# Attention weights and V split in two parts each: three fp32r matmuls where one fp32 matmul stood

## The chip, the cores and the metric

One core of a Trainium2 chip runs the whole program. The metric is the device time of one execution in microseconds (us). Three runs of the kernel before took 3181.44, 3177.22 and 3178.43 us; the median is 3178.43 us.

## The reference, cut to what matters

Two layers of a hybrid block over 256 context and 1024 latent tokens, width 1024. Each layer projects the normalised tokens once and feeds three mixers side by side: a Fourier mixing, grouped-query attention (8 query heads, 2 key and value heads of width 64) and a gated linear recurrence (HGRN2); a SwiGLU follows. The change is in this part:

```python
def attend(q, k, v):
    s = jnp.einsum('bkgqd,bksd->bkgqs', q, k).astype(jnp.float32) * (HEAD_DIM ** -0.5)
    p = jax.nn.softmax(s, axis=-1).astype(v.dtype)
    return jnp.einsum('bkgqs,bksd->bkgqd', p, v)
```

Everything is fp32. The latent queries read all 1280 keys; the context queries (layer 0 alone) read the 256 context keys.

## The kernel before, in words

Activations lie with channels on partitions and tokens along the free axis, in blocks of 256 (context), 512 and 512 tokens. Most products are made of two parts per operand: a number is cast to fp32r (the high part), the rest after the cast is the low part, and three fp32r matmuls high·high, high·low and low·high are summed in PSUM (`mm3`, L131 to L133). `split` (L124, L125) makes the parts: ScalarE casts, VectorE subtracts. A few products are single fp32 matmuls, among them `pv`, the product of the exponentials with V (L639).

A layer first runs its projections in order: some gates, the values (`values`, L533), the keys (`keys`, L512 to L518), the queries of four head pairs (`queries`, L562, L563), the other gates. Each block of keys and queries passes `qk_norm_rope`: ScalarE squares it into `qsq` (L470) and scales it into `qraw` (L472), TensorE sums squares (`qss`, L476), ScalarE makes the reciprocal root `qr` in two steps (L311, L312), VectorE turns the block by `sin` and `cos` (L483 to L485). Then a query is multiplied by `qr` and stored to DRAM by a DMA on SyncE's queue (L562, L563); a key is multiplied into `kro` (L512) and split from there into the tiles K1 and K2 of two groups (L516 to L518). In layer 0 VectorE also adds up modulation vectors in the background meanwhile (L274, tiles `as` and `wa`).

Then come the attention units, one for a head pair and a block of queries: twelve in layer 0 (eight of ten steps, four of two), eight of ten steps in layer 1, so 168 steps. A step takes 128 keys: four matmuls `sc` (L630, L631) for two heads, two exponentials on ScalarE (L633), and the two `pv` matmuls of the step before it. Between them stand pieces of other work, handed out at a fixed rate: the next unit's row maxima (`mx`, L597, reduced on VectorE), the recurrence (`lp`, `kv`, `ho` and others) and the Fourier mixing (`pq`, `fo`).

A scheduler puts all instructions in one order for each engine and hands out the buffers of each pool in turn. Two pools matter: `five` has 25 slots of 128x1280 fp32, and `t2` has five slots of 128x512 (`qsq`, `qraw`, `qr` and `kro` among others). While the queries are made, the slots of `five` hold 16 tiles of the normalised tokens (high and low), 2 of V, `cos` and `sin`, and 4 of K1 and K2: 24 in all.

Of the kernel before, what the change touches and what calls it, by code (L numbers as in the profile page):

```python
# [10 lines left out]
F32 = mybir.dt.float32  # L11
F32R = mybir.dt.float32r
U8 = mybir.dt.uint8
AF = mybir.ActivationFunctionType
ALU = mybir.AluOpType
# [3 lines left out]
P = 128  # L19
# [80 lines left out]
class Kern:  # L100
# [434 lines left out]
    def values(self, l):  # L535

        nc = self.nc
        W = 384
        wh, wl = self.wv

        self.V = [self.five(f"V{l}_{g}", shape=(P, 10, P)) for g in range(2)]
        for V in self.V:
            nc.gpsimd.memset(V[:, :, 64:P], 1.0)
        for t in range(10):
            acc = self.ps("mm", f"v{l}_{t}")
            ts = slice(t * P, (t + 1) * P)
            self.mm3(acc[:, :W], [(self.hh[k][:, ts], self.hl[k][:, ts], wh[k], wl[k]) for k in range(KD)])
            for g in range(2):
                nc.scalar.copy(out=self.V[g][:, t, 0:64], in_=acc[:, 64 * g:64 * g + 64])
            vi = self.t2("vi")  # L550
            nc.vector.tensor_copy(out=vi[:, 0:256], in_=acc[:, P:W])
            nc.sync.dma_start(out=self.dv[t], in_=vi[:, 0:256])
# [62 lines left out]
    def unit_attend(self, l, j, ci, Q1, Q2):  # L615


        nc = self.nc
        g = j // 2
        n = CHUNKS[ci][1]  # L620
        nk = 2 if ci == 0 else 10
        pv = [self.ps("pv", f"pv{j}_{ci}_{a}") for a in range(2)]
        ps = []
        for kt in range(nk + 1):
            if kt < nk:
                ks = slice(kt * P, (kt + 1) * P)
                p = []
                for a in range(2):
                    sc = self.ps("sc", "sc")
                    nc.tensor.matmul(sc[:, :n], self.K1[g][:, ks], Q1[a], start=True, stop=False)  # L630
                    nc.tensor.matmul(sc[:, :n], self.K2[g][0:66, ks], Q2[a][0:66], start=False, stop=True)  # L631
                    pf = self.t2(f"p{a}", tag="pa", bufs=PAB)[:, :n]
                    nc.scalar.activation(out=pf, in_=sc[:, :n], func=AF.Exp, scale=0.125)  # L633
                    p.append(pf)
                ps.append(p)
            if kt:
                i = kt - 1
                for a in range(2):
                    nc.tensor.matmul(pv[a][:, :n], self.V[g][:, i], ps[i][a], start=(i == 0), stop=(i == nk - 1))  # L639
            if kt == DELAY and self.pending:  # L640
                self.pending()
                self.pending = None
            yield
        if self.pending:
            self.pending()
        pvs, r = [self.t2(nm, tag="acc", bufs=ACB)[:, :n] for nm in ("pvs", "lns")]
        for a in range(2):
            nc.scalar.copy(out=pvs[64 * a:64 * a + 64], in_=pv[a][0:64, :n])
            nc.scalar.activation(out=r[64 * a:64 * a + 64], in_=pv[a][64:P, :n], func=AF.Ln)
        self.pending = lambda: self.unit_finish(j, ci, pvs, r)  # L650
# [871 lines left out]
```

## Time and profile before

| | |
|---|---|
| median of three runs | 3178.43 us |
| profiled execution | 3176.16 us, span 3174.2 us |
| granted clock | 0.986 of full speed |
| TensorE (PE) busy | 3048.2 us, 96% |
| VectorE (DVE) busy | 1976.1 us, 62% |
| ScalarE (ACT) busy | 1414.2 us, 45% |
| GpSimd (POOL) busy | 114.0 us, 4% |
| attention of layer 0 | first `pv` 347.8 us, last 731.6 us |
| attention of layer 1 | first `pv` 2018.0 us, last 2367.0 us |

The profiled execution lies 2.3 us under the median; about 2 us lie outside its span. Shares of busy time are means over stages with different limits, so each stage is read by its own window. A matmul of fp32 stands in the rows as two records, and the record of a matmul is longer than its distance to the next one, because matmuls are pipelined: the distance between two starts tells what one costs.

### The profile page before, as it was taken

The numbers are of one execution on the slowest core, as the hardware profiler recorded it, in microseconds if no ns is written. First come the engines' busy times: TensorE is split into PE (matmuls) and PEld (weight loads), VectorE is DVE, ScalarE is ACT, GpSimd is POOL, SyncE is SP. The second block draws the span as 40 slices with busy tenths as digits, with TensorE's granted clock in tenths as the row PEclk, the third lists the DMA queues.
The fourth block names the chain that finished last, engine by engine and source line by source line (L and its number), as shares of the span: only waits on it lengthen the run. The fifth ranks groups of instructions, "written<-read, shape, count | busy, mean of one in ns | idle before, by whom it ended". The sixth has DMA issues, their size and how long they took to land.

```text
span 3174.2 us, 43396 instructions
## 1 busy us (share of the span) xinstructions
PE 3048.2 (96%) x16114; PEld 2378.9 (75%) x16114; DVE 1976.1 (62%) x3457; ACT 1414.2 (45%) x2578; POOL 114.0 (4%) x89
## 2 busy tenths in 40 slices
PE   7999999999889999998998999999999799999998
PEld 4877666667768888886888897665668588887887
DVE  5299877663777766665537427777544866666343
ACT  6255555563542323333425535545563433334343
POOL 1000000000210000000001000000001100000000
PEclk9999999999999999998999999999999899999999
DMA  8346201135223333347735423211243122225452
GB/s 290 97 155 206 89 25 67 30 122 172 87 83 100 110 126 111 96 134 231 220 113 179 143 94 105 67 59 36 73 141 118 58 80 81 85 80 189 139 170 93
DMA packets 358651, 369.41 MB, mean 116 GB/s; under 512 B 21896, under 2 KB 268072, under 8 KB 358440
## 3 DMA queue, kind: packets, MB, share of 16 engines
q1 hardware_dynamic: 358440, 366.65, 36.4%
q8 instruction: 126, 2.06, 0.3%
q14 instruction: 85, 0.70, 0.1%
HBM read 282.00 MB, written 84.41 MB: 115 GB/s over the span
## 4 chain that ended last, share of the span: by engine, by line
PE 81%; DVE 8%; ACT 4%; DMA 4%; issue 2%; SPq 1%; POOL 0%; DVEq 0%; ACTq 0%; POOLq 0%
PE fp L131 8%; PE fp L133 8%; PE fp L132 8%; PE pv L639 7%; PE fd L131 5%; PE fd L132 5%; PE fd L133 5%; PE u L131 3%; PE u L132 3%; PE u L133 3%; PE mx L597 2%; PE sc L630 2%; PE sc L631 2%; PE oacc L132 2%; PE oacc L131 2%; PE oacc L133 2%
## 5 line engine op out<-in xcount | busy, mean ns | idle before, releaser
L131 PE MATMUL fd<-a,hwd 128*128 128x512 f32 (+1 forms) x880 | 328.3, 373 | 16.5 <-ACT hwd L124 16.5
L133 PE MATMUL fd<-a,lwd 128*128 128x512 f32 (+1 forms) x880 | 327.9, 373 | 8.9 <-DVE lwd L125 8.9
L132 PE MATMUL fd<-a,hwd 128*128 128x512 f32 (+1 forms) x880 | 327.0, 372 | 0.0
L125 DVE TENSOR_TENSOR lwd<-rwd,hwd 128x512 fp32r<-128x512 f32 (+1 forms) x240 | 158.1, 661 | 269.1 <-ACT hwd L124 260.3
L639 PE MATMUL pv<-p,V 128*128 128x512 f32 (+1 forms) x672 | 316.0, 584 | 0.0
L124 ACT CAST hwd<-rwd 128x512 fp32r<-128x512 f32 (+1 forms) x240 | 140.3, 585 | 306.6 <-PE fd L132 178.7
L598 DVE TENSOR_REDUCE mp<-mx 128x1 f32<-128x512 f32 (+1 forms) x400 | 220.7, 589 | 69.2 <-PE mx L597 66.1
L633 ACT ACTIVATE p<-sc 128x512 f32<-128x512 f32 (+1 forms) x336 | 184.1, 585 | 132.5 <-PE sc L631 128.7
L131 PEld LDWEIGHTS fd<-a,hwd 128*128 128x128 f32 x880 | 168.9, 192 | 45.1 <-ACT hwd L124 17.4
L133 PEld LDWEIGHTS fd<-a,lwd 128*128 128x128 f32 x880 | 168.3, 191 | 38.4 <-DVE lwd L125 10.9
L132 PEld LDWEIGHTS fd<-a,hwd 128*128 128x128 f32 x880 | 168.9, 192 | 27.7 <-issue 0.2
L274 DVE SCALAR_TENSOR_TENSOR as<-wa,sc,as 128x512 f32<-128x512 f32 x224 | 161.1, 747 | 36.3 <-DMA wa<-in_w_ada_dram 34.9
L639 PEld LDWEIGHTS pv<-p,V 128*128 128x128 f32 x672 | 122.7, 189 | 77.9 <-issue 62.7
L131 PE MATMUL fp<-mh,hw_gate 128*128 128x512 f32 x352 | 141.2, 401 | 6.1 <-ACT hw_gate L124 6.0
L133 PE MATMUL fp<-mh,lw_gate 128*128 128x512 f32 x352 | 139.5, 396 | 5.8 <-DVE lw_gate L125 5.8
L132 PE MATMUL fp<-ml,hw_gate 128*128 128x512 f32 x352 | 139.4, 396 | 1.2 <-POOL ml L1051 1.2
L131 PE MATMUL fp<-mh,hw_up 128*128 128x512 f32 x352 | 137.8, 392 | 0.0
L132 PE MATMUL fp<-ml,hw_up 128*128 128x512 f32 x352 | 137.8, 391 | 0.0
L133 PE MATMUL fp<-mh,lw_up 128*128 128x512 f32 x352 | 137.2, 390 | 0.0
L131 PE MATMUL u<-a0hh,hwin 128*128 128x512 f32 (+1 forms) x360 | 132.3, 370 | 3.9 <-ACT a0hh L327 2.1
L132 PE MATMUL u<-a0hl,hwin 128*128 128x512 f32 (+1 forms) x360 | 129.1, 359 | 5.5 <-POOL a0hl L325 3.8
L133 PE MATMUL u<-a0hh,lwin 128*128 128x512 f32 (+1 forms) x360 | 127.3, 355 | 0.0
(353 smaller groups left out, 7376.8 us busy)
## 6 DMA issues: line engine op xcount, KB each, us to landing
rwd<-in_w_down_dram SPq DMA_DIRECT2D x200, 256.0 KB
wa<-in_w_ada_dram SPq DMA_DIRECT2D x192, 256.0 KB
rw_gate<-in_w_gate_dram SPq DMA_DIRECT2D x44, 512.0 KB
rw_up<-in_w_up_dram SPq DMA_DIRECT2D x44, 512.0 KB
da<-mw_gate SPq DMA_DIRECT2D x88, 256.0 KB
ar<-da SPq DMA_DIRECT2D x88, 256.0 KB
rwin<-in_w_in_dram SPq DMA_DIRECT2D x30, 512.0 KB
rwo<-in_w_out_dram SPq DMA_DIRECT2D x24, 512.0 KB
```

The lines of the kernel that those rows point to most:

```text
L124: self.nc.scalar.copy(out=hi, in_=src)
L125: self.nc.vector.tensor_tensor(out=lo, in0=src, in1=hi, op=ALU.subtract)
L131: self.nc.tensor.matmul(out, lh, rh, start=(first and i == 0), stop=False)
L132: self.nc.tensor.matmul(out, lh, rl, start=False, stop=False)
L133: self.nc.tensor.matmul(out, ll, rh, start=False, stop=(last and i == n - 1))
L274: nc.vector.scalar_tensor_tensor(out=acc, in0=w, scalar=sc, in1=acc, op0=ALU.mult, op1=ALU.add)
L597: nc.tensor.matmul(mx[:, :kn], Q1[a][:, t * P:(t + 1) * P], self.K1[g][:, k0:k0 + kn])
L598: nc.vector.tensor_reduce(out=mp[:, a * nt + t, i:i + 1], in_=mx[:, :kn], axis=AX.X, op=ALU.max)
L630: nc.tensor.matmul(sc[:, :n], self.K1[g][:, ks], Q1[a], start=True, stop=False)
L631: nc.tensor.matmul(sc[:, :n], self.K2[g][0:66, ks], Q2[a][0:66], start=False, stop=True)
L633: nc.scalar.activation(out=pf, in_=sc[:, :n], func=AF.Exp, scale=0.125)
L639: nc.tensor.matmul(pv[a][:, :n], self.V[g][:, i], ps[i][a], start=(i == 0), stop=(i == nk - 1))
```

## The change

V is kept as a high and a low tile per group (four tiles of the pool `five` per layer in place of two; the columns of ones that make the sums of the exponentials get zeros in the low part). `split` fills them: to ScalarE's copy of 128x64 comes a subtract on VectorE, 40 times. Each exponential tile gets a cast on ScalarE and a subtract on GpSimd, 336 times each, written to a new tile `ps` from `five`; `mm3` then replaces the matmul L639. After the edit lines below L546 move by one, those below L635 by four.

```diff
--- before.py
+++ after.py
@@ -538,15 +538,16 @@
         W = 384
         wh, wl = self.wv
 
-        self.V = [self.five(f"V{l}_{g}", shape=(P, 10, P)) for g in range(2)]
+        self.V = [[self.five(f"V{p}{l}_{g}", F32R, (P, 10, P)) for p in "hl"] for g in range(2)]
         for V in self.V:
-            nc.gpsimd.memset(V[:, :, 64:P], 1.0)
+            for v, x in zip(V, (1.0, 0.0)):
+                nc.gpsimd.memset(v[:, :, 64:P].bitcast(F32), x)
         for t in range(10):
             acc = self.ps("mm", f"v{l}_{t}")
             ts = slice(t * P, (t + 1) * P)
             self.mm3(acc[:, :W], [(self.hh[k][:, ts], self.hl[k][:, ts], wh[k], wl[k]) for k in range(KD)])
             for g in range(2):
-                nc.scalar.copy(out=self.V[g][:, t, 0:64], in_=acc[:, 64 * g:64 * g + 64])
+                self.split(acc[:, 64 * g:64 * g + 64], *[v[:, t, 0:64] for v in self.V[g]])
             vi = self.t2("vi")
             nc.vector.tensor_copy(out=vi[:, 0:256], in_=acc[:, P:W])
             nc.sync.dma_start(out=self.dv[t], in_=vi[:, 0:256])
@@ -631,12 +632,15 @@
                     nc.tensor.matmul(sc[:, :n], self.K2[g][0:66, ks], Q2[a][0:66], start=False, stop=True)
                     pf = self.t2(f"p{a}", tag="pa", bufs=PAB)[:, :n]
                     nc.scalar.activation(out=pf, in_=sc[:, :n], func=AF.Exp, scale=0.125)
-                    p.append(pf)
+                    y = self.five(f"ps{a}", F32R, (P, 2, 512))
+                    p.append([y[:, i, :n] for i in range(2)])
+                    nc.scalar.copy(out=p[a][0], in_=pf)
+                    nc.gpsimd.tensor_tensor(out=p[a][1], in0=pf, in1=p[a][0], op=ALU.subtract)
                 ps.append(p)
             if kt:
                 i = kt - 1
                 for a in range(2):
-                    nc.tensor.matmul(pv[a][:, :n], self.V[g][:, i], ps[i][a], start=(i == 0), stop=(i == nk - 1))
+                    self.mm3(pv[a][:, :n], [(*[v[:, i] for v in self.V[g]], *ps[i][a])], i == 0, i == nk - 1)
             if kt == DELAY and self.pending:
                 self.pending()
                 self.pending = None
```

The four tiles of V, with the others, make 26 tiles for the 25 slots while the queries are made. The first place is ScalarE in layer 1, where the keys end and the queries begin; K_1_1 is K1 or K2 of the second group, K_1_0 of the first. Before:

```order
L472 ACTIVATE qraw<-u_256_1_17320,colv 128x512
L516 CAST K_1_0_17163<-kro 64x512
L518 CAST K_1_0_17165<-kro 64x512
L516 CAST K_1_1_17164<-kro 64x512
L518 CAST K_1_1_17166<-kro 64x512
L311 ACTIVATE qr<-qss,eps 128x512
L124 CAST hwin_512_0_17505<-rwin_512_17503 128x4x64
L312 ACTIVATE qr<-qr 128x512
L124 CAST hwin_512_0_17505<-rwin_512_17503 128x4x64
L124 CAST hwin_512_4_17511<-rwin_512_17503 128x4x64
```

After, the same place:

```order
L124 CAST hwin_384_4_18345<-rwin_384_18337 128x4x64
L312 ACTIVATE qr<-qr 128x512
L516 CAST K_1_0_18091<-kro 64x512
L518 CAST K_1_0_18093<-kro 64x512
L518 CAST K_1_1_18094<-kro 64x512
L470 ACTIVATE qsq<-u_256_1_18248 128x512
L472 ACTIVATE qraw<-u_256_1_18248,colv 128x512
L124 CAST hwin_512_0_18433<-rwin_512_18431 128x4x64 x2
```

and the end of the last query:

```order
L311 ACTIVATE qr<-qss,eps 128x512
L312 ACTIVATE qr<-qr 128x512
L470 ACTIVATE qsq<-u_640_2_18579 128x512
L472 ACTIVATE qraw<-u_640_2_18579,colv 128x512
L516 CAST K_1_1_18092<-kro 64x256
L516 CAST K_1_1_18092<-kro 64x512 x2
L311 ACTIVATE qr<-qss,eps 128x512
L312 ACTIVATE qr<-qr 128x512
L674 ACTIVATE lsa<-u_1152_0_18629 128x256
```

The cast into K1 of the second group (L516) moved from beside the other three to a place behind the last query's `qsq` and `qraw`; it stands there three times (x2 counts two blocks), with its subtract on VectorE (L517). The slot that it waits for is that of `sin`. In layer 0 it is the same.

The second place is VectorE in layer 0's queries, one block of 512 from the product with `qr` to the rope of the next. Before:

```order
L125 TENSOR_TENSOR lwin_640_4_2161<-rwin_640_2152,hwin_640_4_2160 128x4x64
L276 TENSOR_SCALAR as_2049<-wa_0_6_1828,sc_149 128x512
L276 TENSOR_SCALAR as_2050<-wa_0_7_1874,sc_149 128x512
L276 TENSOR_SCALAR as_2051<-wa_0_7_1874,sc_149 128x512
L274 SCALAR_TENSOR_TENSOR as_2049<-wa_1_6_1890,sc_149,as_2049 128x512
L483 TENSOR_TENSOR qsq<-qraw,sin_1489 64x512 x2
L274 SCALAR_TENSOR_TENSOR as_2050<-wa_1_7_1918,sc_149,as_2050 128x512
L484 TENSOR_TENSOR qraw<-qraw,cos_1488 128x512
L305 SCALAR_TENSOR_TENSOR mod_495<-adat_2027,colv 128x4
L485 TENSOR_TENSOR qraw<-qraw,qsq 128x512
L305 SCALAR_TENSOR_TENSOR mod_495<-adat_2027,colv 128x4
L562 TENSOR_TENSOR qraw<-qraw,qr 128x512
```

After:

```order
L563 TENSOR_TENSOR qraw<-qraw,qr 128x512
L274 SCALAR_TENSOR_TENSOR as_2072<-wa_7_6_2306,sc_149,as_2072 128x512
L274 SCALAR_TENSOR_TENSOR as_2073<-wa_7_6_2306,sc_149,as_2073 128x512
L274 SCALAR_TENSOR_TENSOR as_2074<-wa_7_7_2322,sc_149,as_2074 128x512
L274 SCALAR_TENSOR_TENSOR as_2075<-wa_7_7_2322,sc_149,as_2075 128x512
L276 TENSOR_SCALAR as_2604<-wa_0_8_2364,sc_149 128x512
L274 SCALAR_TENSOR_TENSOR as_2604<-wa_1_8_2431,sc_149,as_2604 128x512
L483 TENSOR_TENSOR qsq<-qraw,sin_1513 64x512 x2
L274 SCALAR_TENSOR_TENSOR as_2604<-wa_2_8_2484,sc_149,as_2604 128x512
L484 TENSOR_TENSOR qraw<-qraw,cos_1512 128x512
L274 SCALAR_TENSOR_TENSOR as_2604<-wa_3_8_2633,sc_149,as_2604 128x512
L485 TENSOR_TENSOR qraw<-qraw,qsq 128x512
```

More of the modulation sums (L274) stand between two blocks of queries. Between the first and the last query's product stand 69 rows of L274 and L276 now, before it was 44; later, among the gates, stand 32 where 60 stood.

The third place is the end of the last unit of layer 0, on TensorE. Before:

```order
L639 MATMUL pv_2_0_6900<-p_6990,V_1_1185 128x512
L639 MATMUL pv_2_1_6901<-p_6995,V_1_1185 128x512
L630 MATMUL sc<-Q_6264,K_0_1_1493 128x512
L631 MATMUL sc<-Q_6265,K_0_1_1495 128x512
L630 MATMUL sc<-Q_6264,K_0_1_1493 128x512
L631 MATMUL sc<-Q_6265,K_0_1_1495 128x512
L639 MATMUL pv_2_0_6900<-p_7002,V_1_1185 128x512
L639 MATMUL pv_2_1_6901<-p_7007,V_1_1185 128x512
L639 MATMUL pv_2_0_6900<-p_7014,V_1_1185 128x512
L639 MATMUL pv_2_1_6901<-p_7019,V_1_1185 128x512
```

After:

```order
L131 MATMUL pv_2_0_7704<-ps_7884,Vh_1_1186 128x512
L132 MATMUL pv_2_0_7704<-ps_7884,Vh_1_1186 128x512
L133 MATMUL pv_2_0_7704<-ps_7884,Vl_1_1187 128x512
L131 MATMUL pv_2_1_7705<-ps_7892,Vh_1_1186 128x512
L132 MATMUL pv_2_1_7705<-ps_7892,Vh_1_1186 128x512
L133 MATMUL pv_2_1_7705<-ps_7892,Vl_1_1187 128x512
L131 MATMUL pv_2_0_7704<-ps_7906,Vh_1_1186 128x512
L131 MATMUL pv_2_1_7705<-ps_7914,Vh_1_1186 128x512
L132 MATMUL pv_2_0_7704<-ps_7906,Vh_1_1186 128x512
L133 MATMUL pv_2_0_7704<-ps_7906,Vl_1_1187 128x512
L132 MATMUL pv_2_1_7705<-ps_7914,Vh_1_1186 128x512
L133 MATMUL pv_2_1_7705<-ps_7914,Vl_1_1187 128x512
```

and ScalarE there, after:

```order
L634 ACTIVATE p_7882<-sc 128x512
L634 ACTIVATE p_7890<-sc 128x512
L637 CAST ps_7884<-p_7882 128x512
L637 CAST ps_7892<-p_7890 128x512
L634 ACTIVATE p_7904<-sc 128x512
L634 ACTIVATE p_7912<-sc 128x512
L637 CAST ps_7906<-p_7904 128x512
L637 CAST ps_7914<-p_7912 128x512
```

Two `sc` pairs still stand ahead of the products of the step before. In each step ScalarE's two casts follow its two exponentials, and at the unit's end no `sc` follows, and the low part of the last tile is an operand of the last matmul but one.

## Rows read from the trace of the kernel before

**Rows 1.** the page, TensorE's busy time (share of the span, instructions)

```profile
PE 3048.2 (96%) x16114; PEld 2378.9 (75%) x16114; DVE 1976.1 (62%) x3457; ACT 1414.2 (45%) x2578; POOL 114.0 (4%) x89
```

**Rows 2.** layer 0's attention by form: count | busy, mean ns | idle

```profile
L639 PE MATMUL pv<-p,V 128*128 128x512 f32 x320 | 154.8, 594 | 0.0
...
L633 ACT ACTIVATE p<-sc 128x512 f32<-128x512 f32 x158 | 88.6, 595 | 63.6 <-PE sc L631 62.5
```

**Rows 3.** one line, the product with V: ns min/median/max, first and last start

```profile
L639 PE MATMUL pv<-p,V x672: 377/592/697, 347.8 to 2368.2; 128*128 128x512 f32 x160, 128*128 128x256 f32 x8
```

**Rows 4.** chain of waits near 650 us: start, us, what

```profile
649.96 1.72 PE pv L639 x4
```

**Rows 5.** timeline of TensorE, end of layer 0's attention: start, us, what

```profile
712.41 1.88 PE L639 MATMUL pv<-p,V 128*128 128x512 f32 x4
...
714.37 0.39 PE L631 MATMUL sc<-Q,K 66*128 66x512 f32 x1
...
714.60 0.40 PE L630 MATMUL sc<-Q,K 128*128 128x512 f32 x1
...
715.07 1.88 PE L639 MATMUL pv<-p,V 128*128 128x512 f32 x4
...
729.87 3.60 PE L639 MATMUL pv<-p,V 128*128 128x512 f32 x8
```

**Rows 6.** windows: length, busy PE, PEld, DVE, ACT, POOL, clock, DMA share, GB/s

```profile
110.00:165.00 55.00, 54.72 (x309) 52.69 (x308) 14.60 (x31) 12.29 (x40) 0.00 (x0) 1.00 0.30 97
192.00:255.00 63.00, 61.47 (x302) 48.56 (x302) 62.21 (x109) 31.83 (x62) 0.00 (x0) 1.00 0.54 168
255.00:345.00 90.00, 88.44 (x446) 71.31 (x447) 77.19 (x144) 49.30 (x91) 0.41 (x1) 1.00 0.60 200
340.00:740.00 400.00, 390.75 (x2715) 250.90 (x2715) 275.10 (x596) 242.40 (x449) 4.55 (x4) 1.00 0.24 77
1900.00:1963.00 63.00, 62.83 (x270) 48.63 (x268) 47.99 (x78) 35.81 (x66) 0.00 (x0) 1.00 0.24 76
```

**Rows 7.** TensorE's waits in layer 0's attention: us in total, times, longest

```profile
PE sc L630 <- ACT p L633: 3.0, 4, 1.3
```

**Rows 8.** ScalarE's groups by form, the cast of 128x512

```profile
L124 ACT CAST hwd<-rwd 128x512 fp32r<-128x512 f32 x200 | 124.0, 620 | 240.0 <-PE fd L132 122.1 <-DMA rwd<-in_w_down_dram 100.0 <-PE fd L133 9.1
```

**Rows 9.** GpSimd's groups by form, two inputs of 128x512

```profile
L392 POOL TENSOR_TENSOR sqa<-sqa,sq 128x512 f32<-128x512 f32 x20 | 29.0, 1452 | 346.1 <-ACT sq L391 346.1
L1096 POOL TENSOR_TENSOR xT<-xT,xT 128x512 f32<-128x512 f32 x8 | 16.5, 2070 | 37.6 <-ACT xT L1046 37.6
L1051 POOL TENSOR_TENSOR ml<-xT,mh 128x512 fp32r<-128x512 f32 x8 | 13.5, 1694 | 0.1
```

**Rows 10.** timeline of VectorE, one block of queries in layer 1

```profile
1909.61 1.39 DVE L483 TENSOR_TENSOR qsq<-qraw,sin 64x512 f32<-64x512 f32 x2
...
1912.09 0.69 DVE L485 TENSOR_TENSOR qraw<-qraw,qsq 128x512 f32<-128x512 f32 x1
```

**Rows 11.** timeline of ScalarE, the same blocks

```profile
1908.89 0.69 ACT L472 ACTIVATE qraw<-u,colv 128x512 f32<-128x512 f32 x1
...
1909.48 0.68 ACT L311 ACTIVATE qr<-qss,eps 128x512 f32<-128x512 f32 x1
...
1910.34 0.64 ACT L312 ACTIVATE qr<-qr 128x512 f32<-128x512 f32 x1
```

**Rows 12.** timeline of TensorE, square sums of two blocks

```profile
1906.70 1.02 PE L476 MATMUL qss<-qsq,c_blkq 128*128 128x512 f32 x2
...
1913.02 1.02 PE L476 MATMUL qss<-qsq,c_blkq 128*128 128x512 f32 x2
```

**Rows 13.** timeline of SyncE, a query's store in layer 0

```profile
232.29 0.33 SPq L563 DMA_DIRECT2D dq<-qraw  x1
```

**Rows 14.** timeline of ScalarE, what waited for that store

```profile
234.29 0.47 ACT L472 ACTIVATE qraw<-u,colv 128x256 f32<-128x256 f32 x1 [0.41 <-DMA dq<-qraw]
```

**Rows 15.** VectorE's groups by form in layer 0's queries

```profile
L274 DVE SCALAR_TENSOR_TENSOR as<-wa,sc,as 128x512 f32<-128x512 f32 x39 | 28.0, 747 | 0.3
```

## The prediction

> **What bounds the kernel now.** I read the page first: TensorE is busy for 96% of the span, GpSimd for 4% [rows 1]. So a change pays if it shortens TensorE's work and nothing else comes late. Next I read the stages by window, since the change touches four: the values, the queries of each layer, and the attention of each layer. In the attention of layer 0 TensorE is busy 390.75 of 400 us, VectorE 275 and ScalarE 242 [rows 6], and TensorE's waits for the exponentials come to 3.0 us in all [rows 7]. The reader is to see that the products with V stand on the path, and also that ScalarE has 158 us to spare there, not more. In the queries of layer 0 two engines are full at once: VectorE 62.21 and TensorE 61.47 of 63 us; in layer 1 it is TensorE alone, 62.83 of 63, with VectorE at 47.99 [rows 6].
>
> **The products.** Four records in a row, two for each fp32 matmul, take 1.72 us in the chain, so one product with V costs 0.86 us [rows 4]. An fp32r matmul of 128x512 starts 0.23 us after the one before (714.37 to 714.60) [rows 5]. Three make 0.69 to 0.70. The saving is 0.165 us on each of 320 products of 512 columns (the line's 672 records are 336 products, 16 of them of 256 columns [rows 3]), and about half on the 16: 54 us of TensorE's time. That is the gain if no product waits.
>
> **ScalarE's casts and GpSimd's subtracts.** A cast costs 0.62 us [rows 8], an exponential 0.595 [rows 2]. For two heads a step then needs 2.43 us of ScalarE, and 320 casts are 198 us more of it, some 105 of them in layer 0: its 242 of 400 us become about 347, in a stage meant to shrink. GpSimd's operation with two inputs took 1.45 us in the mean, 1.69 where it made a low part, and 2.07 in the worst group [rows 9]. I take 1.45, the row with the most instructions: two per step are 2.9 us, so GpSimd becomes the longest engine of a step with nothing else in it. Such a step takes 2.66 us now (712.41 to 715.07 [rows 5]) and would need 2.33 of TensorE after the change.
>
> The Trainium skill bears on that span: "SBUF — State Buffer", section "SBUF: two separate sides", says that VectorE with two SBUF inputs and GpSimd share one pair of ports under an exclusive lock, the loser blocked for the whole instruction. By that rule each overlap would add a whole VectorE instruction of 0.69 us to GpSimd, or the reverse. The rows agree in direction (1.45 against 1.69 and 2.07); in the attention, where many of VectorE's instructions are row maxima out of PSUM, I expect the low end. If the rule bit on every subtract, it would give the second rival below.
>
> Three places pay for this.
> - *Steps with little other work.* I counted the distances between starts of L639: of 166 inside the two stages 20 are 2.5 to 2.7 us, 6 between 2.0 and 2.5, 21 between 2.7 and 3.3. With a floor of 2.9 us instead of 2.33 to 2.97 they lose about 20 us against the full saving. With GpSimd undisturbed at 1.3 (below its means, so the low bound) it is 8; at 1.7 and a floor of 3.4, 47.
> - *Ends of units.* Now the last two steps' products follow one another (eight records in a row at 729.87 [rows 5]). After the change the last low part comes late: from the start of the last scores 0.47 us, two exponentials and two casts to 2.9, GpSimd's two subtracts, begun at 2.3, to 5.2, and two matmuls to 5.7 us. TensorE's own work there is 0.94 + 4 x 0.69 = 3.7. So 2.0 us are open, filled in part by maxima and pieces of the recurrence: I take 1.6 for 16 units of ten steps and 0.7 for the four short ones, 28 us (12 if mostly filled, 45 at GpSimd's 1.7).
> - *Thick steps.* ScalarE at some 90% delays the recurrence's and the maxima's evictions now and then, and GpSimd's reads hold VectorE up. No row shows how much; TensorE's present waits of 3.0 us [rows 7] are the lower end, 30 us the upper (0.18 us for each of 168 steps, a quarter of one VectorE instruction of 0.69). I take 8, near the row.
>
> Attention: -54 + 20 + 28 + 8 = +2 us. The gain in TensorE's work is eaten by the chain exponential, cast, subtract.
>
> **Values.** 40 subtracts of 128x64 come to VectorE, which is busy 14.6 of 55 us there [rows 6]; at most 0.43 us each by the cost of 256 columns (half of 0.69, rounded up for the start), 17 us in both layers, under TensorE's 54.72. Nothing; without that cover it would be these 17.
>
> **The queries, through the slots.** This does not stand in the diff's lines. Four V tiles make 26 tiles for 25 slots, so K1 of the second group waits for the slot of `sin`, which is free after the last query's rope; the order shows its cast moved there. Until then three `kro` blocks are held in three of the five `t2` slots, and `qsq`, `qraw` and `qr` of every query share two. So the next block's `qraw` cannot start before this block's store has landed, and `qr` not before `qsq` has been added. The chain per block of 512 is: the store, 232.29 to the start of what waited for it at 234.29, 2.0 us [rows 13, 14]; `qraw` 0.69 and the two steps of `qr` 0.68 and 0.64 [rows 11]; rope 1.39, cosine and sum 0.69 each, the product as long, 0.69 [rows 10]; together 7.5, with some eight handovers of about 0.06 us 8.0. Now a block takes 6.32 us (1906.70 to 1913.02 [rows 12]), TensorE's time. Layer 1 has eight blocks: 1.65 x 8 = 13, less what the two accumulators buffer: +12 us (6 to 16).
>
> In layer 0 the same chain meets a full VectorE, onto which the order puts 25 more sums between the first and the last query's product; at 0.747 us [rows 15] they are 19 us, with more latency around them. Later, among the gates, 28 fewer stand, but there TensorE is the limit (88.44 of 90 us, VectorE 77.19 [rows 6]), so this gives nothing back. +20 us (5 if the two-slot chain leaves VectorE room for the sums, 33 if chain and sums add).
>
> **Start of the recurrence.** Its tiles also come from the pool of 25 and now load when the last projection has let go of its inputs, five loads at once as the attention begins. Pieces of work handed out in the first steps wait; 0 to 15 us, I take 3, since TensorE has the maxima and scores in front of them.
>
> **Sum.** 3176.2 us of the profiled execution + 2 + 12 + 20 + 3 = 3213; the profiled run lies 2.3 us under the median, so 3215 us. All terms at their low ends give 3176 - 54 + 12 + 8 + 0 + 6 + 5 = 3153, all at their high ends 3308.
>
> **Rivals.**
> 1. *The chain hides and the kernel gets faster.* GpSimd stays at 1.3 us, since VectorE's work there reads PSUM, and the maxima and the recurrence fill the ends of units. For it: only 47 of 166 distances are under 3.3 us and TensorE is in order with other work in most steps. Against it: the end of layer 0's attention has seven bare steps in a row and each unit's end has nothing behind it in the order. The attention would gain 54 - 12 - 8 = 34, the queries cost at most 11 as VectorE's sums slip between: 3155 us with the 2.3. It decides if layer 1's attention, 2018 to 2369 now, falls under 335 us.
> 2. *GpSimd bounds the attention.* Each subtract at 1.7 us and VectorE's instructions blocked in turn: steps under 3.4 us vanish, 47 + 45 + 20 - 54 = +58, with the queries 3271 us. For it: 1.69 in the group that did the same operation [rows 9]. Against it: the most frequent group is at 1.45.
> 3. *The queries do not stall* (the slots' order costs nothing because the accumulators run ahead), and only the attention's +2 remains: 3181, no change. Against it: two accumulators cover one block, and there are eight.
>
> **How the numbers follow.** The forecast with its sum has 0.56 (own range 3190 to 3245), rival 1 0.2, rival 2 0.14, rival 3 0.1. A measurement of this kernel can tell about 0.2%, 6.4 us. The forecast lies above 3185 for nearly all its part; rival 3 is mostly inside. So faster 0.2, same 0.1, slower 0.7. The range reaches a little past rival 1's 3155 and to rival 2's 3271, 3148 to 3275: the outer halves of both lie outside, with some room since their terms are bounds and not means.
>
> **What would show it.** Right: `qss` of layer 1 about 8 us apart instead of 6.32; `qraw` waiting for the DMA; layer 0's queries ending 15 to 30 us later; in the attention TensorE waiting for GpSimd's L638 at the end of each unit for 1 to 2 us; bare steps of 2.8 to 3.0; attention stages as long as now within 10 us. Wrong: `qss` still 6.3 us apart, or the attention shorter by 40 us in the two layers with no wait for L638, or subtracts far from 1.3 to 1.7 us.

## The result, and the profile after

The changed kernel takes 3402.05 us (four runs, 3387.47 to 3404.59) against 3179.93 for the kernel before in the same comparison: a ratio of 1.0685, 95% interval 1.0671 to 1.0699, so about 218 us slower (213 to 222). The prediction said slower, but 3215 us, and its range ended at 3275.

From the first and last starts of the groups on TensorE in the two traces, the span is split into stages; idle is the time in which TensorE ran nothing.

| stage (us) | before | after | difference | idle before | idle after |
|---|---|---|---|---|---|
| layer 0: keys and queries (`qss`, first to last) | 81.7 | 118.5 | +36.8 | 2.6 | 22.8 |
| layer 0: attention (`pv`) | 385.0 | 468.8 | +83.8 | 9.2 | 66.1 |
| layer 0: output projection (last `pv` to first `fp`) | 113.2 | 127.3 | +14.1 | 0.4 | 6.1 |
| layer 1: keys and queries (last `v` to last `qss`) | 68.0 | 84.8 | +16.8 | 0.2 | 11.9 |
| layer 1: attention | 350.2 | 410.5 | +60.3 | 9.1 | 55.7 |
| layer 1: output projection | 87.9 | 93.6 | +5.7 | 0.1 | 2.7 |
| all else | 2088.2 | 2095.0 | +6.8 | | |

The page of the changed kernel, the engines' busy time and the granted clock in 40 slices, beside [rows 1]:

```profile
PE 3128.1 (92%) x16450; PEld 2484.0 (73%) x16450; DVE 2071.4 (61%) x3497; ACT 1591.7 (47%) x2914; POOL 564.1 (17%) x429
...
PEclk9989989998999999998999999999989999999999
```

TensorE is busy 80 us longer, though its work became less. The windows of the changed kernel (length, busy time of PE, PEld, DVE, ACT, POOL, granted clock, DMA share, GB/s) answer to [rows 6]: the two query stages, the two attentions, and 20 us inside the first attention:

```profile
166.00:285.00 119.00, 96.22 (x406) 70.50 (x404) 101.47 (x169) 43.30 (x81) 0.00 (x0) 0.90 0.46 141
2034.00:2115.00 81.00, 69.13 (x282) 49.94 (x280) 45.63 (x74) 34.92 (x64) 0.00 (x0) 1.00 0.17 56
386.00:854.00 468.00, 401.96 (x2808) 286.38 (x2806) 313.34 (x570) 313.02 (x590) 230.91 (x178) 0.90 0.15 46
2177.00:2588.00 411.00, 355.28 (x2380) 253.33 (x2380) 257.29 (x463) 278.81 (x498) 226.19 (x164) 0.92 0.16 52
...
496.00:506.00 10.00, 7.02 (x43) 4.56 (x41) 9.92 (x14) 9.86 (x18) 5.31 (x4) 1.00 0.00 0
506.00:516.00 10.00, 10.00 (x52) 6.92 (x52) 4.63 (x9) 3.66 (x7) 4.12 (x4) 0.55 0.08 28
```

Read the clock column: 1.00 in the attention before, 0.90 and 0.92 after. In the last two rows VectorE and ScalarE are full while TensorE waits 3 of 10 us at the upper level; in the next 10 us TensorE is full, but mostly at the lower of its two levels (0.55, 1.2 GHz and not 2.4). So a wait seems to be paid for twice here, and this is no single case: the two attentions hold 21 stretches at the lower level, and in the 10 us ahead of one TensorE had been idle for 2.7 us in the mean, against 1.4 in the mean of all such 10 us.

What TensorE waited for in layer 0's attention (us in total, times, longest), beside the 3.0 us of [rows 7] (all its waits together came to 9.2 before):

```profile
PE pv L132 <- POOL ps L638: 18.5, 37, 0.9
PE pv L131 <- ACT ps L637: 11.8, 2, 8.4
PE lp L793 <- DVE atc L800: 8.8, 6, 3.0
PE mx L598 <- DVE mp L599: 6.8, 11, 1.7
PE fo L131 <- ACT yh L124: 4.1, 1, 4.1
PE lp L768 <- DVE kk L741: 4.0, 2, 3.1
PE sc L631 <- ACT p L634: 3.8, 5, 1.7
```

Only the first row and part of the second are the chain that the prediction priced. The others are the recurrence, the maxima and the Fourier mixing behind VectorE and ScalarE. VectorE's groups by form there (count | busy, mean ns) show why:

```profile
L599 DVE TENSOR_REDUCE mp<-mx 128x1 f32<-128x512 f32 x112 | 73.0, 684 | 27.6 <-PE mx L598 27.1
L817 DVE TENSOR_TENSOR W<-W,G 128x256 f32<-128x256 f32 x48 | 35.1, 754 | 3.4 <-PE lp L793 3.2
L819 DVE TENSOR_TENSOR hk<-hk,G 128x640 f32<-128x640 f32 x24 | 30.0, 1252 | 0.1
...
L853 DVE SCALAR_TENSOR_TENSOR ST<-ST,G,kv 64x64 f32<-64x64 f32 x72 | 20.2, 280 | 17.8 <-PE kv L850 15.3 <-PE mx L598 0.4
```

Before, the same groups took in the mean

```profile
L598 DVE TENSOR_REDUCE mp<-mx 128x1 f32<-128x512 f32 x112 | 73.3, 685 | 28.3 <-PE mx L597 27.5
...
L815 DVE TENSOR_TENSOR hk<-hk,G 128x640 f32<-128x640 f32 x24 | 19.7, 821 | 2.1 <-ACT kk L775 1.9
L813 DVE TENSOR_TENSOR W<-W,G 128x256 f32<-128x256 f32 x48 | 18.6, 416 | 3.0 <-PE lp L789 2.8
```

The maxima read PSUM and kept their time; W and `hk`, with two inputs in SBUF, went from 416 to 754 and from 821 to 1252 ns. These means hide two kinds. Of the 48 W of this form in layer 0's attention, 29 took 398 to 426 ns, as before. The other 19 began while a subtract ran on GpSimd; each of them ended 0.28 to 0.29 us behind the end of that subtract, so they took 622 to 1517 ns, 1273 in the mean. The timeline of the two engines shows it (start, us):

```profile
466.76 0.23 DVE L821 TENSOR_TENSOR G<-G 128x80 f32<-128x80 f32 x1
467.37 1.48 POOL L638 TENSOR_TENSOR ps<-p,ps 128x512 fp32r<-128x512 f32 x1 [2.85 <-ACT ps L637]
467.64 1.83 DVE L817 TENSOR_TENSOR W<-W,G 128x256 f32<-128x256 f32 x2
469.15 1.44 POOL L638 TENSOR_TENSOR ps<-p,ps 128x512 fp32r<-128x512 f32 x1 [0.30 <-ACT ps L637]
469.39 1.30 DVE L821 TENSOR_TENSOR G<-G 128x80 f32<-128x80 f32 x1
```

The same operation on G takes 0.23 us by itself and 1.30 when it begins inside a subtract; of the two W, the first takes 1.49 us and the second 0.41. It goes the other way too: in layer 1 one subtract stood for 4.52 us, while eight operations on W, `hk` and G ran inside it at their usual times. GpSimd's subtract took 1381 ns in the mean there (158 of 128x512, 214.9 us), a little under the 1452 of [rows 9].

The queries of layer 1, TensorE's square sums (start, us), against the 6.32 us of [rows 12]:

```profile
2082.00 1.12 PE L476 MATMUL qss<-qsq,c_blkq 128*128 128x512 f32 x2
2090.21 1.13 PE L476 MATMUL qss<-qsq,c_blkq 128*128 128x512 f32 x2 [0.37 <-ACT qsq L470]
2097.95 1.13 PE L476 MATMUL qss<-qsq,c_blkq 128*128 128x512 f32 x2
```

and ScalarE's start of a block, which waits for the store of the block before:

```profile
2091.54 0.69 ACT L472 ACTIVATE qraw<-u,colv 128x512 f32<-128x512 f32 x1 [0.87 <-DMA dq<-qraw]
```

Blocks are 8.0 us apart (15.95 for two), as worked out.

### The profile page after: what moved, and what is told of

Same layout as the page of the kernel before. It is cut to its first block, busy times and chain, and to the rows that moved or that the text cites. A ratio compares the mean times of both kernels' runs of the same rounds, so it can differ in the third digit from the quotient of the medians.

```text
span 3398.5 us, 45288 instructions
## 1 busy us (share of the span) xinstructions
PE 3128.1 (92%) x16450; PEld 2484.0 (73%) x16450; DVE 2071.4 (61%) x3497; ACT 1591.7 (47%) x2914; POOL 564.1 (17%) x429
## 5 line engine op out<-in xcount | busy, mean ns | idle before, releaser
L638 POOL TENSOR_TENSOR ps<-p,ps 128x512 fp32r<-128x512 f32 (+1 forms) x336 | 451.7, 1366 | 965.7 <-ACT ps L637 564.9
L637 ACT CAST ps<-p 128x512 fp32r<-128x512 f32 (+1 forms) x336 | 191.3, 613 | 2.9 <-PE fo L132 0.6
L132 PE MATMUL pv<-ps,Vh 128*128 128x512 f32 (+1 forms) x336 | 152.6, 454 | 40.7 <-POOL ps L638 38.4
L274 DVE SCALAR_TENSOR_TENSOR as<-wa,sc,as 128x512 f32<-128x512 f32 x224 | 161.4, 754 | 37.0 <-DMA wa<-in_w_ada_dram 36.3
L131 PE MATMUL pv<-ps,Vh 128*128 128x512 f32 (+1 forms) x336 | 143.5, 431 | 21.6 <-ACT ps L637 21.5
L325 POOL TENSOR_TENSOR a1hl<-hf,a1hh 128x512 fp32r<-128x512 f32 (+1 forms) x12 | 15.0, 1247 | 836.6 <-PE fd L133 807.2
L132 PEld LDWEIGHTS pv<-ps,Vh 128*128 128x128 f32 x336 | 67.7, 201 | 99.5 <-POOL ps L638 90.1
```

The lines of the kernel that those rows point to most:

```text
L131: self.nc.tensor.matmul(out, lh, rh, start=(first and i == 0), stop=False)
L132: self.nc.tensor.matmul(out, lh, rl, start=False, stop=False)
L274: nc.vector.scalar_tensor_tensor(out=acc, in0=w, scalar=sc, in1=acc, op0=ALU.mult, op1=ALU.add)
L325: nc.gpsimd.tensor_tensor(out=lo, in0=u, in1=hi, op=ALU.subtract)
L637: nc.scalar.copy(out=p[a][0], in_=pf)
L638: nc.gpsimd.tensor_tensor(out=p[a][1], in0=pf, in1=p[a][0], op=ALU.subtract)
```

## The experiments

All times are medians of the runs of one comparison, the ratios with 95% intervals. The attention is given as the sum of both layers, from the first to the last `pv`: 735.2 us before, 879.3 after.

**Two idle tiles in the kernel before.** Does the shortage of slots explain the queries, and only them?

```diff
+        self.idle = [self.five(f"idle{l}_{g}", shape=(P, 10, P)) for g in range(2)]
+        for V in self.idle:
+            nc.gpsimd.memset(V[:, :, 64:P], 0.0)
 ...
         nc.vector.tensor_tensor(out=r, in0=pvs, in1=r, op=ALU.mult)
+        for V in self.idle:
+            nc.gpsimd.tensor_copy(out=V[:, 0, 0:64], in_=r[:, 0:64])
```

> The kernel before with two more tiles of the pool of 25 slots, held from the values to the last attention unit by a copy of 128x64 on GpSimd at each unit's end; products, casts and subtracts as before. Theory A (the slots cost the queries alone; the attention's loss comes from the chain cast, subtract, product and the lower clock behind it): queries of layer 0 about 37 us longer, of layer 1 about 16, attention within 10 us of before per layer: about 3235 us. Theory B (the missing slots also hold up the tiles of the recurrence and so cause most of the attention's loss): attention at least 30 us longer per layer, above 3290 us.

3229.96 us, ratio 1.0161 (1.0145 to 1.0176): +51.4. Queries 116.2 and 82.8 us (+34.5, +14.8), attention 386.3 and 349.9: unchanged. The slots cost the queries, and nothing in the attention.

**Low parts of V in one tile.** The reverse: give the slot back to the changed kernel.

```diff
-        self.V = [[self.five(f"V{p}{l}_{g}", F32R, (P, 10, P)) for p in "hl"] for g in range(2)]
+        self.V = [self.five(f"Vh{l}_{g}", F32R, (P, 10, P)) for g in range(2)]
+        self.Vl = self.five(f"Vl{l}", F32R, (P, 10, P))
 ...
-                    self.mm3(pv[a][:, :n], [(*[v[:, i] for v in self.V[g]], *ps[i][a])], i == 0, i == nk - 1)
+                    vh, vl = self.V[g][:, i], self.Vl[:, i, 64 * g:64 * g + 64]
+                    nc.tensor.matmul(pv[a][:, :n], vh, ps[i][a][0], start=(i == 0), stop=False)
+                    nc.tensor.matmul(pv[a][0:64, :n], vl, ps[i][a][0], start=False, stop=False)
+                    nc.tensor.matmul(pv[a][:, :n], vh, ps[i][a][1], start=False, stop=(i == nk - 1))
```

> The changed kernel with the low parts of V of both groups in one tile of 64 columns each, so that 25 tiles fill the 25 slots; the product low times high is of 64 columns of V and goes to the upper half of the sums. Theory A: the queries go back to 82 and 64 us, attention stays at about 470 and 410: 3402 - 53 = about 3350 us. Theory B: attention falls back below 410 and 360 us, about 3230.

3322.59 us, ratio 1.0453 (1.0435 to 1.0472), 79 us under the changed kernel. Queries 81.0 and 68.0: all of their loss is back. The attention is 857.2, 22 us better, which was not expected; the high-low product now comes last of the three, which gives GpSimd 0.23 us more. That can be half of it at most: without any subtract the packing alone took the attention from 778.6 to 767.9 us (two runs further down), and why is not shown. Most of the attention's loss stays: theory B is wrong.

**No subtract; a subtract that no product reads.** (Slots as in the changed kernel.)

```diff
-                    p.append([y[:, i, :n] for i in range(2)])
+                    p.append([y[:, 0, :n], y[:, 0, :n]])
                     nc.scalar.copy(out=p[a][0], in_=pf)
-                    nc.gpsimd.tensor_tensor(out=p[a][1], in0=pf, in1=p[a][0], op=ALU.subtract)
```

> The changed kernel without GpSimd's subtract: the middle product takes the high part a second time (so the low part of the exponentials is left out); casts, slots and 1008 matmuls stay. Theory A: with no chain through GpSimd and no port shared with it, TensorE waits little, VectorE's W returns from 754 to 416 ns, the clock to 1.0, and the attention lies 25 to 45 us under before in both layers together; with the queries' 53: about 3200 us. Theory B: no change from 3402 but for a few us.

3289.52 us, ratio 1.0349 (1.0334 to 1.0365); attention 778.6. W is back at 417 ns, as expected, but the attention is 43 us above before and not 25 to 45 below: so the casts cost too.

```diff
-                    p.append([y[:, i, :n] for i in range(2)])
+                    p.append([y[:, 0, :n], y[:, 0, :n]])
                     nc.scalar.copy(out=p[a][0], in_=pf)
-                    nc.gpsimd.tensor_tensor(out=p[a][1], in0=pf, in1=p[a][0], op=ALU.subtract)
+                    nc.gpsimd.tensor_tensor(out=y[:, 1, :n], in0=pf, in1=p[a][0], op=ALU.subtract)
```

> The changed kernel with the subtract kept on GpSimd but read by no product (the middle product takes the high part, so the low part of the exponentials is left out). It tells the wait for the subtract from its load on the ports. If the wait for GpSimd is what costs (A1): as without the subtract, about 3200 to 3230 us. If the slower VectorE behind the shared reads is what costs (A2): W stays at about 750 ns, TensorE waits for VectorE's lp and mp tiles as in the changed kernel, 3320 us or more. Half and half: about 3280.

3361.1 us, ratio 1.0574 (1.0558 to 1.059); attention 848.7. Of the 101 us of attention between no subtract and the changed kernel, 70 come with a subtract for which TensorE never waits, and 31 with waiting for it. A2 holds for the larger part: seven tenths are the load, three tenths the chain.

**Subtract on VectorE.** `nc.gpsimd` becomes `nc.vector` in that line.

> The changed kernel with the subtract on VectorE in place of GpSimd (slots as in the changed kernel). VectorE takes 0.69 us for it where GpSimd takes 1.38, and no port is shared, but VectorE gets 336 more instructions, about 115 us per layer's attention on top of 268 and 234. Theory A2 (what the subtract costs is mostly VectorE slowed down by shared reads): W back at 416 ns, attention of layer 0 about 440, of layer 1 about 385 us, in all about 3350 us. Rival (VectorE's own load decides): VectorE over 90% busy, attention as long as in the changed kernel or longer, 3400 us or more.

3384.88 us, ratio 1.0649 (1.0633 to 1.0665); attention 868.2. W is at 415 ns and VectorE busy for 354 of 450 us in layer 0, 79%: neither expectation held. The port is free, but the work is now in VectorE's own order, and that costs nearly as much: the attention is 11 us shorter.

**Products two steps behind, packed V.**

```diff
-        for kt in range(nk + 1):
+        for kt in range(nk + 2):
 ...
-            if kt:
-                i = kt - 1
+            if kt > 1:
+                i = kt - 2
```

> The packed V (25 tiles for 25 slots) and the products two steps behind the scores in place of one. If TensorE's waits for the cast and the subtract are latency of the chain, these (18 and 20 us by row, some 12 and 10 for the cast) go, and with them part of the low clock: 3322 - 50 = about 3270 us. If the load on ScalarE, VectorE and the ports decides, the waits turn up elsewhere (lp and mx behind VectorE): 3310 us or more.

3330.54 us, ratio 1.0475 (1.046 to 1.0491): no gain, as the second expectation has it. TensorE's wait for the subtract in layer 0 falls from 15.9 to 7.5 us, and its wait for the maxima rises from 8.4 to 17.1. A longer lead moves the waits, it does not remove them.

**Direct exponential.** What are three matmuls worth when nothing else is added?

```diff
-                    pf = self.t2(f"p{a}", tag="pa", bufs=PAB)[:, :n]
-                    nc.scalar.activation(out=pf, in_=sc[:, :n], func=AF.Exp, scale=0.125)
-                    y = self.five(f"ps{a}", F32R, (P, 2, 512))
-                    p.append([y[:, i, :n] for i in range(2)])
-                    nc.scalar.copy(out=p[a][0], in_=pf)
-                    nc.gpsimd.tensor_tensor(out=p[a][1], in0=pf, in1=p[a][0], op=ALU.subtract)
+                    ph = self.t2(f"p{a}", F32R, tag="pa", bufs=PAB)[:, :n]
+                    nc.scalar.activation(out=ph, in_=sc[:, :n], func=AF.Exp, scale=0.125)
+                    p.append([ph, ph])
```

> Packed V, and the exponential written by ScalarE straight as fp32r: no cast, no subtract, still three matmuls per product (the middle one takes the high part again; the low part of the exponentials is left out). It shows what the matmuls alone are worth. Theory A: nothing new is late, TensorE stays at full clock and gives back the whole 54 us: 3178 - 54 = about 3126 us, attention 358 and 325 us. Rival (three matmuls of fp32r do not pay in this place, by weight loads or the clock): 3160 us or more.

3129.0 us, ratio 0.9845 (0.9831 to 0.986), 50 us faster; attention 689.5, 45.7 under before. The windows of its two attentions:

```profile
347.00:709.00 362.00, 351.00 (x2809) 261.38 (x2808) 264.20 (x577) 228.06 (x427) 2.27 (x2) 1.00 0.21 66
1998.00:2325.00 327.00, 314.62 (x2375) 234.41 (x2374) 234.29 (x476) 199.99 (x350) 2.27 (x2) 0.99 0.22 74
```

So the prediction's 54 us were there, but for a few. This run is the floor of the next ones, which add one thing to it at a time; all have packed V.

**Cast alone, read and unread; a short one.** The read cast is the run without the subtract on packed V. The unread one:

```diff
                     p.append([ph, ph])
+                    y = self.five(f"ps{a}", F32R, (P, 2, 512))
+                    nc.scalar.copy(out=y[:, 0, :n], in_=ph)
```

> Packed V, exponentials cast on ScalarE, no subtract (the middle product takes the high part again; the low part of the exponentials is left out). From the unpacked run without the subtract, 3289.5, less the 51 us of the slots: about 3238 us, so 109 us for the casts alone over the direct exponential. If the packing had helped the attention for itself: 3225 or less.

> Direct exponential, and a cast on ScalarE to a tile that no product reads (the low part is left out of the products). ScalarE's load alone, without the chain. If ScalarE's load in its fixed order is what the casts cost (its other copies for the recurrence, the maxima and the Fourier mixing come late): about 3129 + 80 = 3210 us. Rival (the chain exponential, cast, product costs, not the load): 3150 us or less.

3232.04 us, ratio 1.0168 (1.0153 to 1.0183), and 3233.15, with the same ratio and interval. The attention is 767.9 and 767.1: a cast in the chain costs as much as one that nobody waits for, 78 us. So the cast costs as load on ScalarE, and that a product waits for it adds nothing to speak of. (The first of the two lies between its two expectations, 3238 and 3225.) The short one copies 32 columns:

> Direct exponential, and an unread cast of 32 columns in place of 512 on ScalarE (the low part of the exponentials is left out): the same number of instructions, tiles and places in ScalarE's order, a fraction of its time. If the casts cost by their time in ScalarE's order: 3129 + 15 to 35 = about 3150 us. If by the slots of the pool or by places in the order: 3215 us or more.

3198.76 us, ratio 1.0064 (1.0046 to 1.0082); attention 736.2, 47 above the floor, and the time lies between the two expectations. Its group in layer 0 by form:

```profile
L637 ACT CAST ps<-p 128x32 fp32r<-128x32 f32 x174 | 32.0, 218 | 1.1 <-DVE yl L125 0.2
```

A copy of 32 columns still took 218 ns, a third of the 625 of the full one, and cost 60% of what that did. Time on ScalarE alone is not the measure.

**Subtract alone; a memset in its place.**

```diff
                     p.append([ph, ph])
+                    y = self.five(f"ps{a}", F32R, (P, 2, 512))
+                    nc.gpsimd.tensor_tensor(out=y[:, 1, :n], in0=ph, in1=ph, op=ALU.subtract)
```

> Direct exponential without a cast, and a subtract on GpSimd from the exponentials that no product reads (the low part is left out of the products). GpSimd's load alone. If the shared reads are what costs: VectorE's W at about 700 ns, TensorE waiting for lp and mx tiles, 3129 + 60 to 70 = about 3195 us. Rival (the load hurts only where ScalarE is full as well): 3145 us or less.

3272.96 us, ratio 1.0302 (1.0283 to 1.032); attention 804.3, 115 above the floor (144 in the whole time, where 60 to 70 were expected), with ScalarE's work unchanged. Then `nc.gpsimd.memset(y.bitcast(F32), 0.0)` in place of the subtract:

> Direct exponential, and on GpSimd a memset of the 128x1024 tile in place of the unread subtract (the low part of the exponentials is left out): as many instructions of nearly 1 us on GpSimd and the same tiles from the pool, but nothing read from SBUF. If the subtract's cost is the reads that it shares with VectorE: W of VectorE at 416 ns, about 3129 to 3145 us. If it is the tiles of the pool (slots that the recurrence waits for) or GpSimd's time as such: 3220 us or more.

3161.65 us, ratio 0.9947 (0.9931 to 0.9964); attention 693.8, 4 above the floor. VectorE and GpSimd in layer 0, first with the subtract, then with the memset:

```profile
L821 DVE TENSOR_TENSOR hk<-hk,G 128x640 f32<-128x640 f32 x24 | 27.5, 1150 | 0.0
L819 DVE TENSOR_TENSOR W<-W,G 128x256 f32<-128x256 f32 x48 | 27.2, 593 | 1.0 <-PE lp L795 0.9
...
L637 POOL TENSOR_TENSOR ps<-p 128x512 fp32r<-128x512 f32 x148 | 174.4, 1199 | 205.2 <-ACT p L634 155.8 <-ACT yh L124 39.3 <-DVE zb L957 4.1
```

```profile
L821 DVE TENSOR_TENSOR hk<-hk,G 128x640 f32<-128x640 f32 x24 | 19.5, 818 | 0.1
L819 DVE TENSOR_TENSOR W<-W,G 128x256 f32<-128x256 f32 x48 | 18.7, 417 | 0.3 <-PE lp L795 0.3
...
L637 POOL MEMSET ps<- 128x1024 f32 x168 | 151.8, 951 | 210.0 <-PE kdt L848 52.1 <-DVE zo L963 45.2 <-PE lp L795 35.1
```

GpSimd is busy nearly as long (152 and 174 us), and the tiles of the pool are the same, but nothing is read: VectorE keeps its speed and the attention its gain. 22 of the 48 W ran beside a memset, and they took 417 ns as the others did. The memset differs in one thing more: it waits for no exponential and holds no exponential's buffer. That is small, since ScalarE waited 4.1 us in all for the subtract in layer 0. So the subtract costs by its reads, which hold VectorE up. (The run is 33 us above the floor elsewhere: 21 us of it stand in the output projections, where TensorE waits for the casts of `mh`.)

**Fillers for the clock.** In the packed kernel a matmul of zeros before each product:

```diff
+                    if i:
+                        nc.tensor.matmul(pv[a][0:32, :n], self.zero, Q1[a], start=False, stop=False)
                     vh, vl = self.V[g][:, i], self.Vl[:, i, 64 * g:64 * g + 64]
```

> The packed kernel (3323 us) with one matmul of zeros, 32 columns by the block's 512, added to the sums before each product but the first of a unit: 304 more fp32r matmuls, about 70 us of TensorE's work in the two attentions, in places where it waited 68 and 53 us. It tells whether the lower granted clock (0.93, 0.94 there) follows from those waits. If it does: clock 0.97 or more in both attentions, the 74 us that the same matmuls took longer than in the run without casts shrink by half or more, and the time is 3290 to 3325 us, no longer than without the fillers. If the clock has another cause: clock stays at 0.93 and the fillers cost 30 to 70 us, 3355 to 3390.

3336.93 us, ratio 1.0499 (1.0483 to 1.0514), 14 us over the packed kernel, with 296 fillers (the expectation counted 304). The clock rose from 0.93 to 0.96 in layer 0, where the attention grew by 2 us for 152 fillers of at most 0.23 us (35 us of work), and stayed at 0.94 in layer 1, where it grew by 17 for 144 (33 us). That is between the two expectations: it speaks for the clock following the waits in layer 0. Layer 1 does not speak against it, since TensorE was still idle for 42 us there, and in the 10 us ahead of each of its seven stretches at the lower level for 2.8 us in the mean, against 1.0 in all of the stage. The run does not settle it.

**Two products.** The direct exponential with two matmuls, high and low part of V, per product (the middle one left out).

> As the direct exponential, with two matmuls per product, high and low part of V times the rounded exponentials (the low part of the exponentials is left out). Theory A: 0.86 - 0.46 = 0.40 us less for each of 320 products, 130 us of TensorE's work; ScalarE (234 of 385 us) and VectorE (268) then are closer to the bound, so 100 to 130 of it arrive: 3050 to 3080 us. Rival (the attention is then held by VectorE and by the order): 3110 us or more.

3074.58 us, ratio 0.9675 (0.9659 to 0.9691): 104 us faster than before and the best of all. It computes less than the change does, since the exponentials are rounded to fp32r once; the sums of the softmax are taken from the same rounded numbers.

## Why the prediction was wrong

In the two traces the changed kernel is 224 us longer: 54 in the queries, 144 in the attention, 20 in the output projections and 7 in all else. The prediction had 32, 2, nothing and 3.

**The products (-54)** were nearly right: 45.7 us in the attention of the direct exponential, 50 in the whole time.

**The queries (+12 and +20)** were right in mechanism and short in size: +16.8 and +36.8, and +14.8 and +34.5 with the idle tiles alone. Layer 1's blocks are 8.0 us apart as worked out. In layer 0 the term was given as 5 to 33, with 33 "if chain and sums add", and the measured time lies a little above that. In its window VectorE is busy 101 of 119 us, TensorE idle for 22.8, and the clock at 0.90, for which there was no term.

**The chain (+20 for bare steps, +28 for ends of units)** was right in kind and too large: TensorE waits 18.5 and 20.0 us for the subtract in the two layers, and the kernel that reads the subtract is 31 us of attention above the one that doesn't, where the prediction had 48. The waits are also not the predicted ones of 1 to 2 us at each unit's end: in layer 0 they are 37, the longest 0.9 us. Bare steps at the end of layer 0 take 2.5 to 3.4 us (products start at 841.32, 843.92, 847.31 and 849.80), where the prediction had 2.8 to 3.0.

**The step that failed is "Thick steps"**: "I take 8, near the row", with 30 as the upper end. It started from the 3.0 us of the kernel before, which are the waits for the exponentials alone (all waits came to 9.2), left even these out of its lowest sum, and took a ScalarE at some 90% and a VectorE at 275 of 400 us for nearly free. The runs show what stands in its place. Over the floor of 689.5 us a cast that nobody reads costs 78, a subtract that nobody reads 115, and both together, with the subtract unread, 159 (848.7; the unpacked V is in that, some 11 us). So the load on the other engines costs about 150 us where the term had 8, over three times the gain. The upper end, a quarter of one VectorE instruction per step, stood on no row.

**The lock's price was put at the low end.** The prediction wrote that if the rule of the Trainium skill ("SBUF — State Buffer", section "SBUF: two separate sides") bit on every subtract, this would be its second rival, and it expected the low end because many of VectorE's instructions read PSUM. These did keep their time (684 ns, also the 66 of them beside a subtract). But W and `hk` lie on the recurrence's path between two of TensorE's groups, and TensorE's work stands in one order: 19 of 48 W came 0.2 to 1.1 us late, and that holds up all that stands behind `lp`. The trace agrees with the rule: in layer 0 a W that began during a subtract ended only after it, and three that began just before one took 414 to 416 ns. It agrees on the memset as well: for a VectorE operation with two SBUF inputs the rule names only GpSimd operations that read SBUF, and the memset left W at 417 ns.

**The clock was missing.** In the attentions of the packed kernel and of the direct exponential TensorE has the same number of matmuls, and the first takes 168 us more. Idle time went from 23.4 to 122.4 us: 99 more. Busy time went from 665.6 (clock 1.00 and 0.99) to 734.6 (windows of 456 and 401 us, 387.4 and 347.2 busy, clock 0.93 and 0.94): 69 more. By the trace's records of the clock the lower level held for 106 us of the packed kernel's windows, with TensorE busy for 90 of them, and for 7 us in the direct exponential. At the lower level the same work takes up to twice as long (matmuls of 256 columns start 0.21 us apart and not 0.12, in the run without the subtract), so up to half of the 90 us was lost to it: 45, against 3. That makes some 42 of the 168 us, a quarter (an estimate from these rows). The other 27 us of busy time are not shown to be the clock's. Waits too short to show between records that are longer than the distance of starts are the candidate: where no product reads the low part of the exponentials (the unread subtract: 734 us busy, 139 of them at the lower level), the same sum leaves 664 and so nothing over. That the clock follows the waits is seen in the traces (496 to 516 us, and the 21 stretches); the fillers support it in one layer only.

**No term stood for the output projections**, and they took 20 us more. Every run with the `ps` tiles has this: 220 to 227 us for the two, against 201 to 212 in those without them. The tiles, which take slots of `five` up to the end of the attention, are the candidate; no run tested it.

**The rivals.** Rival 2 named GpSimd and VectorE blocking one another, but priced it at 58 us by GpSimd's pace; GpSimd itself was idle half of the time (230.91 of 468 us busy). Rivals 1 and 3 are refuted by the stage table.

**Open**: why a copy of 218 ns on ScalarE costs 47 us when one of 625 costs 78, while GpSimd's memset at the same tiles costs 4. The places in ScalarE's fixed order are the candidate; no run separates them from its time. The waits point there: of TensorE's 47 more us of idle time with the unread cast, 25 stand before pieces of the Fourier mixing (`pq`, `fo`) that ScalarE or VectorE delivers late, and 17 of 34 with the short one.

## What to carry to other kernels

An engine that is 70% busy beside a full TensorE is not free: its instructions lie in a fixed order between TensorE's own, and what they come late by is waited for in order. Before work is moved off TensorE, price it with a run that adds the load and lets nobody read it; here that would have shown 78 and 115 us against a gain of 54. When the load is GpSimd work that reads SBUF, list VectorE's operations with two SBUF inputs beside it: in layer 0's attention every W that began during a subtract waited for its end. And when tiles are added to a pool, count the tiles alive at each stage: one too many cost 51 us far from the edit.

## What the runs showed of the hardware

- VectorE's W, with two SBUF inputs, ended 0.28 to 0.29 us behind the end of GpSimd's subtract when it began during one (19 of 48 in layer 0's attention), and took 398 to 426 ns otherwise: in the mean 754 ns and not 416. A subtract that stood for 4.52 us had eight such operations run at their usual times inside it. Beside GpSimd's memset of 0.95 us it stayed at 417; VectorE's reductions out of PSUM stayed at 684 beside the subtract.
- Three fp32r matmuls in place of one fp32 matmul of 128x512 gave 45.7 us over 336 products, 0.14 each, near the 0.165 read from starts before the change.
- The granted clock fell to 0.55 in 10 us that followed 10 us with TensorE busy for 7.0; in layer 1's queries, with TensorE busy 69.13 of 81 us, it stayed at 1.00.
